# Last layer's half-heads on four PSUM banks of their own, read from the last state on; late operand parts loaded on SyncE's queue

## The chip, the cores and the metric

The kernel runs on one core of a Trainium2 chip. The metric is the time of one execution on the device in microseconds (us), the median over runs. TensorE (PE) multiplies matrices into PSUM, VectorE (DVE) and ScalarE (ACT) read and write PSUM and SBUF, GpSimd (POOL) does small vector work and issues DMAs, and SyncE (SP) only issues DMAs. Each engine works through its own list of instructions in order; semaphores tie the lists together.

## The reference

Two layers (DEPTH 2), 512 frames, width 2048, all in float32. Each layer is

```python
h = rmsnorm(x, g_pre)
z = h @ w_in          # gated linear attention q,k,v,gate,decay; chunk attention q,k,v,gate
...
S_c = diag(a_c) * S_(c-1) + sum over the chunk of decay * k_s v_s^T    # 8 chunks of 64 frames
o_gla = rmsnorm_per_head(q_c S_c) * silu(gg)                           # 4 heads, dk 128, dv 256
o_att = rmsnorm_per_head(chunk attention with bias) * silu(ag)         # 8 heads of 128
y = concatenate([o_gla, o_att]) @ w_out                                # 2048 x 2048
return x + rmsnorm(y, g_post)
```

The state recurrence runs over the chunks, and every frame of chunk c reads the state after its own chunk.

## The kernel before

**Products.** A float32 operand is split into a high and a low part (type fp32r), and each product takes three matmuls (high by high, high by low, low by high; L527 for the projections). A weight tile of 128x1024 comes by DMA into a buffer `raw` or `H` (L184, issued by SyncE), ACT casts its high part `wh` (L261), DVE subtracts for the low part `wl` (L267). There are four buffers each of `raw`, `H` and `wh` and three of `wl`, so the `wl` of one weight tile can be made only when PE is done with the tile three places earlier. Two column blocks of 512 form a pair, whose 2x2 block product is computed in Strassen's way with seven products P1 to P7 in place of eight; each needs a sum of weight tiles (DVE L250 or L253) or a sum of activations (S1 to S4, L1508). One job is one product of one chunk of 256 rows of the inner dimension: 12 matmuls of 128x512.

**The end of the program.** The last layer's output projection consists of the pairs W01 and W23. Its order is fixed by hand: P1 of W23, P1 of W01, P2 of W23, P2 of W01, each over the four chunks in the order 2, 3, 0, 1 (`C_END`); then for W01 P5, a mix of P6 and P3, P7 and P4; then the same for W23. The P1s need only the attention half of the activations. The P2s need the gated linear attention for the first 256 frames, and P5 on need it for all frames and the sums S1 to S4.

**Units.** The gated linear attention is done in eight half-heads, called units here, u0 to u7 in this order of (head, half of the frames): (0,0), (1,0), (2,0), (3,0), (2,1), (3,1), (0,1), (1,1). A unit has six steps. `outer` (L1300): four products k by v of 128x256 on PE into two PSUM banks. `states` (DVE L1320, L1322): four steps of the recurrence out of these banks. `read` (L1338): four products of q by state into a third bank. `norm` (ACT L1348 squares, POOL L1353 and L586 the power). `gate` (DVE L1360). `turn`: four transposes on PE (L1370) into a fourth bank, scaled by ACT (L1381) and split into high and low (ACT L113, DVE L114). All PSUM banks for this come one by one from a ring of four (`aux`), which the attention's last steps use as well. `gla_line` (L1429) starts unit n+1 while unit n is being read; it is a generator, advanced by a number of steps after every job (`rate`).

**Sums.** For each of the four chunks, `paired_sums` (L1479) makes S1, S2, S4 and S3 on DVE (L1508) from the parts of the activations: `parts[c]` has three tiles that `load_parts` reads back from DRAM (L1474 two loads from the attention, L1477 one from the gated linear attention), and the fourth is what `turn` left in SBUF. Each sum is split (ACT L113, DVE L114). S1 and S3 stay in SBUF; S2 and S4 are written to DRAM by POOL (L1522) and read back by SyncE (L238) shortly before P6 and P3. Chunks 2 and 3 are the early ones, 0 and 1 the late ones. Sums may begin when the states of all eight units have been issued (L1486).

**Loads.** The early parts are loaded on SyncE's queue after P1 of W23, into buffers `sa`. The late parts are loaded on POOL's queue after the last P1 of W01, into the buffers `a110` to `a113`, which are free when PE has done that P1. The gains for the output's norm (L1584) are on POOL's queue as well.

**What opens P5.** P5 of W01 writes the two banks that P2 of W23 filled. So ACT squares these banks (L1594) and DVE multiplies them by the gain (L1597) before P5's first matmuls; and the first weight sum of P5 (L250, called opening in L249) is tied behind that multiplication.

**Order.** The program is written in one order and then placed: for each engine a scheduler chooses the next instruction by its own idea of the times, held back by `tc.issue_after` where the kernel says so. So an edit of the written order changes the order on an engine only by way of this scheduler, and what stands where is read from the finished lists.

Of the kernel before, what the change touches and what calls it, by code (L numbers as in the profile page):

```python
# [35 lines left out]
def hybrid_trunk(  # L36
# [13 lines left out]
    nc = tc.nc  # L50
# [842 lines left out]
    def layer(l):  # L893
# [380 lines left out]
        og, og_full, issued = {}, {}, {"outer": 0, "states": 0}  # L1274
# [3 lines left out]
        class Unit:  # L1278
# [10 lines left out]
            def outer(self):  # L1289
                h, p = self.h, self.p  # L1290
                hk = slice(h * P, (h + 1) * P)
                hv = slice((h % 2) * 256, (h % 2 + 1) * 256)
                self.ps_u = [aux(), aux()]
                nc.vector.memset(self.ps_u[0][:, 0:1], 0.0)
                mm = None
                for tt in (1, 0):
                    for cc in (1, 0):
                        r = slice(cc * 64, (cc + 1) * 64)
                        with tc.issue_after(mm) if mm else nullcontext():
                            mm = nc.tensor.matmul(  # L1300
                                self.ps_u[cc][:, tt * 256 : (tt + 1) * 256], kd[p][r, tt, hk], self.gv[p][r, tt, hv],
                                start=True, stop=True,
                            ).ins
                issued["outer"] += 1
# [24 lines left out]
            def read(self):  # L1329
                h, p = self.h, self.p  # L1330
                self.ps_o = aux()
                mm = None
                for tt in range(2):
                    for cc in range(2):
                        q = 2 * tt + cc
                        n = 4 * p + q
                        with tc.issue_after(mm) if paired and mm else nullcontext():
                            mm = nc.tensor.matmul(  # L1338
                                self.ps_o[cc * 64 : (cc + 1) * 64, tt * 256 : (tt + 1) * 256],
                                gqT[h // 2][:, h % 2, n * 64 : (n + 1) * 64], self.st[q],  # L1340
                                start=True, stop=True,
                            ).ins
# [15 lines left out]
            def gate(self):  # L1358
                for tt in range(2):
                    nc.vector.scalar_tensor_tensor(  # L1360
                        out=self.sg[:, tt, :], in0=self.ps_o[:, tt * 256 : (tt + 1) * 256],
                        scalar=self.r[:, tt : tt + 1], in1=self.sg[:, tt, :], op0=ALU.mult, op1=ALU.mult,
                    )

            def turn(self):
                h, p = self.h, self.p
                ps = aux()
# [59 lines left out]
        units_due = []  # L1427

        def gla_line():  # L1429
            n, older = 0, None  # L1430
            while n < 8 or older is not None:
# [10 lines left out]
                yield  # L1442
# [5 lines left out]
                yield  # L1448
                yield
# [4 lines left out]
                yield  # L1454
                if older is not None:
                    older.gate()
                    delayed.append([4, older.turn])
# [11 lines left out]
        def load_parts(c, tiles):  # L1469
            views = [z.bitcast(F32)[:, i, :] for z in tiles for i in range(2)]  # L1470
            parts[c] = views
            q = nc.sync if c in C_END[:2] else nc.gpsimd
            for half, z in ((0, views[0]), (1, views[1])):
                q.dma_start(  # L1474
                    z.rearrange("p (k n) -> p k n", k=2), of_att[l][c][:, :, half * 256 : (half + 1) * 256]
                )
            q.dma_start(views[2], of_gla[l][0, c])  # L1477

        def paired_sums():  # L1479
# [5 lines left out]
            def ready(name, c):  # L1485
                if issued["states"] < 8 or c not in og_full or c not in parts:  # L1486
# [151 lines left out]
        def paired_out():  # L1638
# [14 lines left out]
            def side(n):  # L1653
                def f(k, c):
# [3 lines left out]
                    if (n, k, c) == (0, "P1", C_END[3]):  # L1658
                        gains[2], gains[0] = load_gain(2, nc.gpsimd), load_gain(0, nc.gpsimd)
                        for i in range(2):  # L1660
# [151 lines left out]
```

## Time and profile before

| | before |
|---|---|
| median of three runs (lowest to highest) | 1629.56 us (1629.43 to 1633.03) |
| profiled execution, its own time | 1631.98 us |
| span of the profiled execution | 1630.2 us |
| mean granted clock of TensorE | 0.992 |
| instructions | 24390 |
| PE busy | 1589.9 us (98% of the span) |
| DVE busy | 1275.6 us (78%) |
| ACT busy | 934.5 us (57%) |
| the last layer's paired output projection and units | about 1360 us on |

The profiled execution took 2.42 us longer than the median; of its 1631.98 us, 1.8 us lie outside the span. The profile's page gives for every engine its busy time and share. Groups of instructions are named by engine, source line, and output and inputs by tile name, with the idle time that the engine had just before them and the engine or DMA that ended this idle time. A row of the timeline has the start, the duration in us, the engine, the line, the operation, the shapes, the count, and in square brackets the idle time before it with what ended it. In the timeline a float32 matmul of a unit counts as two.

### The profile page before, as it was taken

The page shows a single profiled execution, that of the slowest core. Times are in us where ns is not written, and L with a number is a line of the kernel's source. Part 1 is how long each engine was busy: PE and PEld are TensorE (multiplying, and loading weights), DVE is VectorE, ACT ScalarE, POOL GpSimd, SP SyncE. Part 2 cuts the span into 40 slices and gives each one's busy share as a digit, 9 for nine tenths or more (in the row PEclk, how much of TensorE's full clock was granted, in tenths as well). Part 3 has the DMA queues.
Part 4 walks back from the last instruction along what each step waited for, and adds up shares of the span by engine and source line. Part 5 has one row for each costly group of instructions (what it writes and reads, how often), then busy time and mean ns, then how long its engine had stood idle before and what let it go on. Part 6 is the DMA issues. An engine that isn't in the chain of part 4 may idle for free.

```text
span 1630.2 us, 24390 instructions
## 1 busy us (share of the span) xinstructions
PE 1589.9 (98%) x8770; PEld 1347.9 (83%) x8770; DVE 1275.6 (78%) x1590; ACT 934.5 (57%) x1540; POOL 176.5 (11%) x306
## 2 busy tenths in 40 slices
PE   9999999999999999999999999999999999996896
PEld 6777889999988877788878888899998887775675
DVE  6778876877876886688869887868688767769687
ACT  8565544556676535455776455446667665455453
POOL 1131000000001102310121100000000010021101
PEclk9999999999999999999999999999999999998999
DMA  9999966858867797998689987787596848956794
GB/s 376 346 338 342 331 229 242 296 184 315 286 220 263 250 347 246 348 372 329 255 293 331 352 312 267 259 268 274 192 301 219 287 149 289 387 177 238 261 339 168
DMA packets 146857, 459.70 MB, mean 282 GB/s; under 512 B 16188, under 2 KB 34628, under 8 KB 146736
## 3 DMA queue, kind: packets, MB, share of 16 engines
q1 hardware_dynamic: 124560, 381.86, 66.6%
q0 software_dynamic: 21600, 75.33, 12.3%
q8 instruction: 69, 1.13, 0.3%
q10 hardware_dynamic: 576, 0.95, 0.2%
q14 instruction: 52, 0.43, 0.1%
HBM read 392.23 MB, written 64.77 MB: 280 GB/s over the span
## 4 chain that ended last, share of the span: by engine, by line
PE 85%; issue 6%; DMA 5%; DVE 3%; ACT 1%; POOL 1%; SPq 0%; POOLq 0%; DVEq 0%; ACTq 0%
PE mm L527 49%; PE mm L512 20%; PE mm L398 5%; DMA raw<-in_w_dram 3%; PE ax L1128 2%; DMA H<-in_w_dram 1%; DVE wl L267 1%; PE ax L1111 1%; PE ax L1338 1%; PE ax L1300 1%; PE ax L527 1%; PE ax L721 1%; PE ax L1091 1%; PE ax L1090 1%; PE ax L1089 1%
## 5 line engine op out<-in xcount | busy, mean ns | idle before, releaser
L267 DVE TENSOR_TENSOR wl<-raw,wh 128x1024 fp32r<-128x1024 f32 x248 | 302.8, 1222 | 119.7 <-PE mm L527 42.6
L261 ACT CAST wh<-H 128x1024 fp32r<-128x1024 f32 x251 | 263.5, 1052 | 224.2 <-PE mm L527 101.9
L261 ACT CAST wh<-raw 128x1024 fp32r<-128x1024 f32 x248 | 260.9, 1052 | 217.1 <-PE mm L527 98.0
L267 DVE TENSOR_TENSOR wl<-H,wh 128x1024 fp32r<-128x1024 f32 (+1 forms) x253 | 307.6, 1218 | 88.9 <-PE mm L527 35.3
L527 PE MATMUL mm<-wh,sa 128*128 128x512 f32 x1088 | 348.0, 394 | 5.2 <-DMA sa<-oS 4.6
L527 PE MATMUL mm<-wh,g 128*128 128x512 f32 x928 | 290.3, 392 | 6.5 <-ACT wh L261 6.1
L527 PE MATMUL mm<-wh,a 128*128 128x512 f32 x864 | 278.1, 395 | 2.3 <-ACT pc L450 0.9
L527 PEld LDWEIGHTS mm<-wh,sa 128*128 128x128 f32 x1088 | 203.9, 188 | 51.0 <-issue 7.5
L250 DVE TENSOR_TENSOR H<-H,raw 128x1024 f32<-128x1024 f32 x176 | 213.5, 1220 | 29.0 <-DMA raw<-in_w_dram 19.5
L512 PE MATMUL mm<-sa,wh 128*128 128x256 f32 x1280 | 235.9, 285 | 0.0
L527 PE MATMUL mm<-wl,sa 128*128 128x512 f32 x544 | 213.4, 392 | 0.0
L527 PEld LDWEIGHTS mm<-wh,g 128*128 128x128 f32 x928 | 175.2, 189 | 43.5 <-ACT wh L261 6.4
L512 PEld LDWEIGHTS mm<-sa,wh 128*128 128x128 f32 x1280 | 199.4, 191 | 0.3
L527 PEld LDWEIGHTS mm<-wh,a 128*128 128x128 f32 x864 | 160.9, 188 | 42.3 <-issue 5.8
L527 PE MATMUL mm<-wl,g 128*128 128x512 f32 x464 | 182.7, 394 | 11.4 <-DVE wl L267 11.4
L512 PE MATMUL mm<-sa,wl 128*128 128x256 f32 x640 | 180.8, 283 | 0.0
L527 PE MATMUL mm<-wl,a 128*128 128x512 f32 x432 | 169.7, 394 | 1.2 <-DVE wl L267 1.2
L512 PEld LDWEIGHTS mm<-sa,wl 128*128 128x128 f32 x640 | 122.3, 191 | 0.1
L527 PEld LDWEIGHTS mm<-wl,sa 128*128 128x128 f32 x544 | 102.6, 189 | 22.1 <-issue 0.7
L527 PEld LDWEIGHTS mm<-wl,g 128*128 128x128 f32 x464 | 87.6, 189 | 34.4 <-DVE wl L267 16.2
L527 PEld LDWEIGHTS mm<-wl,a 128*128 128x128 f32 x432 | 81.2, 188 | 20.6 <-DVE wl L267 3.0
L512 PE MATMUL mm<-a,wh 128*128 128x256 f32 x512 | 94.5, 285 | 0.0
(229 smaller groups left out, 2027.9 us busy)
## 6 DMA issues: line engine op xcount, KB each, us to landing
raw<-in_w_dram SPq DMA_DIRECT2D x356, 512.0 KB, 5.4
sa<-S SPq DMA_DIRECT2D x128, 512.0 KB, 4.6
H<-in_w_dram SPq DMA_DIRECT2D x67, 512.0 KB, 6.1
S<-g POOLq DMA_DIRECT2D x32, 512.0 KB, 6.2
g<-S SPq DMA_DIRECT2D x32, 512.0 KB, 5.9
sa<-A SPq DMA_DIRECT2D x32, 512.0 KB, 6.0
sa<-oS SPq DMA_DIRECT2D x32, 512.0 KB, 4.8
oS<-g POOLq DMA_DIRECT2D x24, 512.0 KB, 4.4
```

What stands on the lines that cost most here:

```text
L250: nc.vector.tensor_tensor(out=h, in0=h, in1=r, op=ALU.add)
L261: last_cast[0] = nc.scalar.copy(self.wh, src).ins
L267: last_low[0] = nc.vector.tensor_tensor(out=self.wl[:, kk, :], in0=self.src[:, kk, :], in1=self.wh[:, kk, :].bitcast(F32), op=ALU.subtract ...
L398: mm = nc.tensor.matmul(pss[o], a[:, part, t], rhs[:, kk, :], start=(i == 0 and kk == 0 and m == 0), stop=(i == n - 1 and kk == 1 and m == 2),
L512: nc.tensor.matmul(dst, lhs[:, kk, f], a[:, part, tok], start=(fresh and kk == 0 and m == 0 and ft % 2 == 0), stop=(c == self.last and kk ...
L527: mm = nc.tensor.matmul(out_ps[t], a[:, part, tok], rhs[:, kk, :], start=(fresh and kk == 0 and m == 0), stop=(c == self.last and kk == 1 ...
L721: mm = nc.tensor.matmul(gate_ps[l][g : g + 32, half * 256 : (half + 1) * 256], gate_w[l][:, kh * 8 + c * 2 + kk, :], full[half, c][:, kh, ...
L1089: nc.tensor.matmul(ps[:, :n], self.qh[:, t], self.kh[:, :n], start=True, stop=False)
L1090: nc.tensor.matmul(ps[:, :n], self.qh[:, t], self.kl[:, :n], start=False, stop=False)
L1091: nc.tensor.matmul(ps[:, :n], self.ql[:, t], self.kh[:, :n], start=False, stop=True)
L1111: nc.tensor.transpose(ps[:, j * P : (j + 1) * P], self.prob[i][:, j * P : (j + 1) * P], ident)
L1128: nc.tensor.matmul(o, self.pt[i][:, j * P : (j + 1) * P], av[hd // 4, j // 2][:, j % 2, (hd % 4) * P : (hd % 4 + 1) * P], start=(j == 0), ...
```

## The change

Five edits, all in the last layer only, the paired one (`paired` is true there); the lists of the first layer keep their order.

1. **Banks.** Once all four pairs of attention heads are done, `gla_line` takes the whole ring of four auxiliary banks for good. Banks 0 and 1 take every unit's `outer`, bank 2 or 3, by turns, its `read`, and `turn` transposes back into the bank that it was read into. So a unit's `outer` waits for the states of the unit before it, and no unit waits for another user of the ring.
2. **Read order.** `read` goes through the states 3, 2, 1, 0. Its first matmul needs the unit's last state, and the other three need nothing more.
3. **Steps.** Where there is no newer unit to start, `gla_line` leaves out the idle steps that belong to it, and the last `turn` follows its gate after 2 steps and not 4.
4. **Late parts.** The late parts are loaded on SyncE's queue like the early ones, and the loads are written after the first P2 job of W01 and not after the last P1 job.
5. **Sums.** They may begin when the gates of all eight units have been issued, not their states.

```diff
-        og, og_full, issued = {}, {}, {"outer": 0, "states": 0}
+        og, og_full, issued = {}, {}, {"outer": 0, "states": 0, "gates": 0}
...
-                self.ps_u = [aux(), aux()]
+                self.ps_u = gla_banks[:2] if paired else [aux(), aux()]
...
             def read(self):
                 h, p = self.h, self.p
-                self.ps_o = aux()
+                self.ps_o = gla_banks[2 + self.i % 2] if paired else aux()
                 mm = None
-                for tt in range(2):
-                    for cc in range(2):
-                        q = 2 * tt + cc
+                for q in (3, 2, 1, 0) if paired else range(4):
+                    tt, cc = divmod(q, 2)
...
+                issued["gates"] += 1

             def turn(self):
                 h, p = self.h, self.p
-                ps = aux()
+                ps = self.ps_o if paired else aux()
...
-        units_due = []
+        units_due, gla_banks = [], []

         def gla_line():
             n, older = 0, None
+            while len(heads_done) < 4:
+                yield
+            gla_banks.extend(aux() for _ in range(4))
             while n < 8 or older is not None:
...
                 yield
-                yield
+                if newer is not None:
+                    yield
                 if older is not None:
                     older.read()
                 yield
                 if newer is not None:
                     newer.states()
-                yield
-                yield
+                    yield
+                    yield
                 if older is not None:
                     older.norm()
                 yield
                 yield
-                yield
+                if newer is not None:
+                    yield
                 if older is not None:
                     older.gate()
-                    delayed.append([4, older.turn])
+                    delayed.append([4 if newer is not None else 2, older.turn])
...
-            q = nc.sync if c in C_END[:2] else nc.gpsimd
             for half, z in ((0, views[0]), (1, views[1])):
-                q.dma_start(
+                nc.sync.dma_start(
...
-            q.dma_start(views[2], of_gla[l][0, c])
+            nc.sync.dma_start(views[2], of_gla[l][0, c])
...
-                if issued["states"] < 8 or c not in og_full or c not in parts:
+                if issued["gates"] < 8 or c not in og_full or c not in parts:
...
                     if (n, k, c) == (0, "P1", C_END[3]):
                         gains[2], gains[0] = load_gain(2, nc.gpsimd), load_gain(0, nc.gpsimd)
+                    if (n, k, c) == (0, "P2", C_END[0]):
                         for i in range(2):
                             load_parts(C_END[2 + i], [slot(tag, [2, 512], F32R) for tag in (f"a11{2 * i}", f"a11{2 * i + 1}")])
```

In the changed kernel the same operations have other line numbers: `read` is L1337 and no longer L1338, `gate` L1359, the part loads L1478 and L1481 (L1474 and L1477 before), the sums L1512 (L1508), their writes L1526 (L1522), the gain loads L1588 (L1584), the multiplication by the gain L1601 (L1597), the squares L1598 (L1594).

The first place is PE around u2 and u3, in the last pair of the input projection, shortly ahead of P1 of W23. In the names `ax` is a unit's bank, `g_2813` and its like a unit's decayed keys, and `g_2695` the tile `ends`, which holds the last state of each unit of the first half. Before, u2's outer and the first product of u3's stand together, one projection matmul follows, then the rest of u3's:

```order
L1300 MATMUL ax_14050<-g_2813_14045,g_2664_13381 128x256
L1300 MATMUL ax_14049<-g_2813_14045,g_2664_13381 128x256
L1300 MATMUL ax_14050<-g_2813_14045,g_2664_13381 128x256
L1300 MATMUL ax_14049<-g_2813_14045,g_2664_13381 128x256
L1300 MATMUL ax_14085<-g_2813_14045,g_2664_13381 128x256
L527 MATMUL mm_13717<-wh_14039,sa_14043 128x512
L1300 MATMUL ax_14084<-g_2813_14045,g_2664_13381 128x256
L1300 MATMUL ax_14085<-g_2813_14045,g_2664_13381 128x256
L1300 MATMUL ax_14084<-g_2813_14045,g_2664_13381 128x256
L527 MATMUL mm_13717<-wl_14074,sa_14043 128x512
L527 MATMUL mm_13717<-wh_14039,sa_14043 128x512 x2
L527 MATMUL mm_13717<-wl_14074,sa_14043 128x512
```

After, from u3's outer on:

```order
L1300 MATMUL ax_13710<-g_2809_14041,g_2664_13381 128x256
L1300 MATMUL ax_13709<-g_2809_14041,g_2664_13381 128x256
L1300 MATMUL ax_13710<-g_2809_14041,g_2664_13381 128x256
L1300 MATMUL ax_13709<-g_2809_14041,g_2664_13381 128x256
L1337 MATMUL ax_13711<-g_2695_13517,g_2614_13146 64x256
L1337 MATMUL ax_13711<-g_2810_14044,g_2614_13146 64x256 x3
L527 MATMUL mm_13722<-wh_14071,sa_14075 128x512
L527 MATMUL mm_13722<-wl_14105,sa_14075 128x512
L527 MATMUL mm_13722<-wh_14071,sa_14075 128x512 x2
L527 MATMUL mm_13722<-wl_14105,sa_14075 128x512
L527 MATMUL mm_13722<-wh_14071,sa_14075 128x512
L1337 MATMUL ax_13712<-g_2695_13517,g_2614_13146 64x256
```

Behind it, u3's outer is whole, u2's read follows directly, and u3's read follows six projection matmuls later (one row counts two of them) with the product that needs the last state in front. Over all eight units, seven of these groups of four were cut by other instructions before (`outer` of u3, u4 and u6, `read` of u1, u4, u5 and u7), and one is after (`outer` of u6). u7's `turn` stood last ahead of P5; after, 39 projection matmuls stand between it and P5.

The second place is DVE at the start of P5 of W01, up to the first low weight part of P5 that PE waits for. In the names `mm_14396` and `mm_14397` before, and `mm_14374` and `mm_14375` after, are the two banks of W23's P2, `mm_14578` and `mm_14579` (`mm_14550` and `mm_14551`) those of W01's P2; a row with `H` and `raw` is a weight sum, and the last row is P5's first `wl`. Before, directly behind the two L1597 that read W23's banks:

```order
L250 TENSOR_TENSOR H_14366<-H_14366,raw_14768 128x1024
L1508 TENSOR_TENSOR sa_14416<-sa_14416 128x512
L250 TENSOR_TENSOR H_14414<-H_14414,raw_14799 128x1024
L1508 TENSOR_TENSOR sa_14462<-sa_14462 128x512
L250 TENSOR_TENSOR H_14460<-H_14460,raw_14822 128x1024
L1508 TENSOR_TENSOR a_2964_14660<-a_2964_14660 128x512
L250 TENSOR_TENSOR H_14528<-H_14528,raw_14845 128x1024
L114 TENSOR_TENSOR g_2971_14684<-a_2965_14661,g_2971_14684 128x512
L1597 TENSOR_TENSOR g_3007_14870<-mm_14578,t_2963_14658 128x512
L1597 TENSOR_TENSOR g_3009_14874<-mm_14579,t_2963_14658 128x512
L114 TENSOR_TENSOR g_2944_14572<-t_2945_14573,g_2944_14572 128x512
L267 TENSOR_TENSOR wl_14817<-H_14366,wh_14797 128x1024
```

After:

```order
L114 TENSOR_TENSOR g_2906_14498<-t_2907_14499,g_2906_14498 128x512
L1601 TENSOR_TENSOR g_2949_14706<-mm_14374,t_2934_14628 128x512
L1601 TENSOR_TENSOR g_2952_14712<-mm_14375,t_2934_14628 128x512
L250 TENSOR_TENSOR H_14357<-H_14357,raw_14702 128x1024
L1512 TENSOR_TENSOR sa_14394<-sa_14394 128x512
L1512 TENSOR_TENSOR t_2897_14457<-a_2957_14735,t_2897_14457 128x512
L1512 TENSOR_TENSOR t_2907_14499<-a_2959_14740,t_2907_14499 128x512
L250 TENSOR_TENSOR H_14392<-H_14392,raw_14733 128x1024
L1512 TENSOR_TENSOR sa_14433<-sa_14433 128x512
L250 TENSOR_TENSOR H_14431<-H_14431,raw_14779 128x1024
L250 TENSOR_TENSOR H_14486<-H_14486,raw_14817 128x1024
L267 TENSOR_TENSOR wl_14774<-H_14357,wh_14731 128x1024
```

And the rows that follow it, up to P5's second `wl`, where before one L114 stood between the two:

```order
L1512 TENSOR_TENSOR a_2957_14735<-a_2957_14735 128x512
L114 TENSOR_TENSOR a_2961_14746<-sa_14394,a_2961_14746 128x512
L1601 TENSOR_TENSOR g_2979_14842<-mm_14550,t_2935_14630 128x512
L114 TENSOR_TENSOR g_2962_14750<-t_2897_14457,g_2962_14750 128x512
L1601 TENSOR_TENSOR g_2981_14846<-mm_14551,t_2935_14630 128x512
L1512 TENSOR_TENSOR a_2959_14740<-a_2959_14740 128x512
L114 TENSOR_TENSOR g_2963_14754<-t_2907_14499,g_2963_14754 128x512
L267 TENSOR_TENSOR wl_14812<-H_14392,wh_14777 128x1024
```

Between the first of the two multiplications and the first `wl`, twelve operations stood before and nine after; between the first and the second `wl`, one before and seven after. The first sums (L1512) still stand ahead of the gates of u6 and u7 in DVE's list, as before.

The third place is SyncE's queue during the P2s. `sa` takes the early parts, `a` the late parts, `raw` a weight tile. After:

```order
L1481 DMA sa_14434<-fg_191 128x512
L1478 DMA a_2959_14740<-fa_177 128x2x256 x2
L1481 DMA a_2960_14741<-fg_189 128x512
L184 DMA raw_14622<-in_w_dram 128x1024
L1478 DMA a_2957_14735<-fa_176 128x2x256 x2
L184 DMA raw_14648<-in_w_dram 128x1024
L1481 DMA a_2958_14736<-fg_188 128x512
L184 DMA raw_14666<-in_w_dram 128x1024
L184 DMA raw_14684<-in_w_dram 128x1024
```

The four rows with `a` (two of them hold two loads each) stood on POOL's queue before, behind nothing but each other and the units' norms; they now stand among the weight loads. Each must wait for PE to be done with the P1 job that used its buffer.

More of the change, by code (lines that the diff above doesn't have):

```diff
@@ L1330, in read @@
                 h, p = self.h, self.p
-                self.ps_o = aux()
+                self.ps_o = gla_banks[2 + self.i % 2] if paired else aux()
                 mm = None
-                for tt in range(2):
-                    for cc in range(2):
-                        q = 2 * tt + cc
[L1336 to L1342, printed above, removed]
+                for q in (3, 2, 1, 0) if paired else range(4):
+                    tt, cc = divmod(q, 2)
+                    n = 4 * p + q
+                    with tc.issue_after(mm) if paired and mm else nullcontext():
+                        mm = nc.tensor.matmul(
+                            self.ps_o[cc * 64 : (cc + 1) * 64, tt * 256 : (tt + 1) * 256],
+                            gqT[h // 2][:, h % 2, n * 64 : (n + 1) * 64], self.st[q],
+                            start=True, stop=True,
+                        ).ins
             def norm(self):
```

## Prediction

> **What bounds the kernel now.** I read the page first, for the engine with no slack.
>
> ```profile
> PE 85%; issue 6%; DMA 5%; DVE 3%; ACT 1%; POOL 1%; SPq 0%; POOLq 0%; DVEq 0%; ACTq 0%
> ```
>
> PE holds 85% of the chain that ended last, and by the table above it is hardly ever idle. So time can come only from PE's few idle stretches and from PE's own rows. The view of waits, for PE from 1360 us on, the part that the change touches, lists these stretches (total, times, longest):
>
> ```profile
> PE mm L527 <- DVE wl L267: 9.9, 4, 6.4
> PE mm L527 <- ACT wh L261: 6.1, 1, 6.1
> PE mm L527 <- DMA sa<-oS: 4.6, 1, 4.6
> ```
>
> Two waits on DVE and ACT make up 12.6 of some 21 us. The timeline of PE shows where:
>
> ```profile
> 1481.16 0.60 PE L1370 MATMUL ax<-cst,sg 128*128 128x128 f32 x4
> 1487.88 1.22 PE L527 MATMUL mm<-wh,g 128*128 128x512 f32 x2 [6.12 <-ACT wh L261]
> 1495.55 0.79 PE L527 MATMUL mm<-wl,g 128*128 128x512 f32 x1 [6.45 <-DVE wl L267]
> ...
> 1500.16 0.39 PE L527 MATMUL mm<-wl,g 128*128 128x512 f32 x1
> 1500.38 0.39 PE L527 MATMUL mm<-wh,g 128*128 128x512 f32 x1
> 1500.61 0.39 PE L527 MATMUL mm<-wl,g 128*128 128x512 f32 x1
> ...
> 1526.22 0.47 PE L527 MATMUL mm<-wh,sa 128*128 128x512 f32 x1 [4.59 <-DMA sa<-oS]
> ```
>
> P2 of W01 ends with u7's turn at 1481.76; P5 opens 6.12 us later, runs two matmuls, and waits 6.45 us more. Then PE is slow for a while: the 12 matmuls from 1495.55 to 1500.16 take 4.61 us, where at the pace behind 1500.16 (0.45 for two; over whole jobs 0.2275 each) they would take 2.73. The third stop, 4.59 us, is P6's first late operand, which comes back from DRAM. The timeline of DVE tells why the first two are there:
>
> ```profile
> 1484.32 1.29 DVE L1597 TENSOR_TENSOR g<-mm,t 128x512 f32<-128x512 f32 x2 [1.95 <-DMA t<-in_g_post_dram]
> 1485.53 1.21 DVE L250 TENSOR_TENSOR H<-H,raw 128x1024 f32<-128x1024 f32 x1
> ...
> 1494.28 1.22 DVE L267 TENSOR_TENSOR wl<-H,wh 128x1024 fp32r<-128x1024 f32 x1
> ```
>
> The multiplications that free P5's banks start 2.6 us after P2's end, because their gains land late; the first low part of a weight ends only at 1495.5, twelve operations later. From start to start DVE needs 0.60 us for 128x512 (two from 1484.32 to 1485.53) and, as each row ends some 0.08 behind the next one's start, 1.13 for 128x1024. So what counts is when DVE comes to L1597, and how much stands between it and P5's `wl`s.
>
> **The change, part by part.** I call the end of W01's P2 T0: 1481.76 before.
>
> Banks and read order, ahead of T0. The projections go on at 0.2275 us a matmul; what differs is how the units' products lie between them. A group of four that is cut costs more than a whole one:
>
> ```profile
> 1454.60 0.70 PE L1300 MATMUL ax<-g,g 64*128 64x256 f32 x2
> ...
> 1455.65 1.13 PE L1300 MATMUL ax<-g,g 64*128 64x256 f32 x6
> ...
> 1460.14 1.13 PE L1300 MATMUL ax<-g,g 64*128 64x256 f32 x8
> ```
>
> Cut, 0.70 + 1.13 us; whole, 1.13. The 0.70 overlaps the next row by some 0.08, as above, which leaves 0.6 us a cut; a whole group takes 1.05. The order has seven cuts before and one after: -3.6 us. Against that stands a new wait. u3's read now begins with the last state and stands early. The nearest rows are those of the same units before:
>
> ```profile
> 1401.55 1.56 PE L1300 MATMUL ax<-g,g 64*128 64x256 f32 x10
> ...
> 1405.82 0.42 DVE L1320 COPY g<-ax 128x256 f32<-128x256 f32 x1
> 1406.27 1.51 DVE L1322 SCALAR_TENSOR_TENSOR g<-g,a_end,ax 128x256 f32<-128x256 f32 x3
> 1407.70 0.75 DVE L463 SCALAR_TENSOR_TENSOR g<-mm,norm,ev 128x512 f32<-128x512 f32 x1
> 1408.36 1.22 DVE L267 TENSOR_TENSOR wl<-H,wh 128x1024 fp32r<-128x1024 f32 x1
> ```
>
> u2's states are done when u3's copy starts, at 1405.82. Behind them DVE now does L463, a `wl`, L463, the copy, an L250 and three states: 0.66 + 1.13 + 0.66 + 0.45 + 1.13 + 1.43 = 5.5, so u3's last state is there at 1411.3. PE comes from 1401.55 over u2's outer (1.05), 18 matmuls (4.1), u3's outer (1.05), u2's read (as many products, 1.0) and 6 matmuls (1.4) to 1410.1: a wait of 1.2. The units behind it have their own read 27 or more matmuls (6 us) after their outer, against about 2.0 for four states and some 3 for what stands ahead of them on DVE, so I count no wait there. Together -2.4, with -3.6 and 0 as bounds; T0 moves to about 1479.3.
>
> P5's two stops. DVE's order now: the `wl` of the last P2 job can begin when PE has 36 matmuls left, T0 - 8.2, and ends at T0 - 7.1. Then come L114 (which I let wait 0.7 for ACT, a row like that is below), two L1601, L250, three L1512, L250, L1512, two L250 and P5's first `wl`: 0.7 + 0.6 + 1.2 + 1.13 + 1.8 + 1.13 + 0.6 + 2.26 + 1.2 = 10.6. That is T0 + 3.5. The first `wh` comes after the first L250, ahead of T0, so PE does two matmuls (0.45) and stops for 3.1, or 2.4 without the wait for ACT.
>
> ```profile
> 1479.13 1.09 POOL L1584 DMA_DIRECT2D t<-in_g_post_dram  x2
> 1479.58 0.69 DVE L114 TENSOR_TENSOR g<-t,g 128x512 fp32r<-128x512 f32 x1 [0.69 <-ACT g L113]
> 1476.81 0.88 DVE L1360 SCALAR_TENSOR_TENSOR sg<-ax,sm,sg 128x256 f32<-128x256 f32 x2 [0.61 <-POOL sm L586]
> ```
>
> Here the gains must be early. Before, POOL issued them at 1479.13, 2.3 us behind u7's gate, and DVE had them 5.2 us later. Now three `wl`s of P2 stand between u7's gate and L1601, and the first of them can begin at T0 - 8.2 - 2 x 2.73 = T0 - 13.7. So the gate starts by T0 - 14.5, and at the same distances, 2.3 + 5.2, the gains land at T0 - 7.0, 1.2 before L1601 wants them. Without that cover up to the old 1.95 is back.
>
> Up to the second `wl` stand seven operations of 0.60 and itself, 5.4: T0 + 8.9. PE does 10 matmuls and two of the next job, to T0 + 6.25, and stops for 2.65. The third `wl` (1.7 later) is in time, the fourth (4.1 after that, T0 + 14.7) is 0.3 late. Stops 3.1 + 2.65 + 0.3 = 6.05 against 12.57; for two or three short ones while the sums of the late chunks run beside P6 I add 1.1. -5.4, bounds -7 and -3.
>
> The slow stretch cost 4.61 - 2.73 = 1.9 before.
>
> ```profile
> 1480.00:1500.00 20.00, 7.44 (x24) 5.32 (x23) 17.98 (x24) 11.72 (x22) 1.83 (x4) 0.66 0.94 314
> 1561.39 0.50 PE L527 MATMUL mm<-wl,g 128*128 128x512 f32 x1 [1.92 <-DVE wl L267]
> 1561.97 0.39 PE L527 MATMUL mm<-wl,g 128*128 128x512 f32 x1
> ```
>
> The window has a granted clock of 0.66. After the stops of 6.45 and 4.59 the rows are slow, after one of 1.92 they are not. Stops of 3.1 and 2.65 lie between, and I take half of it: -1.0. The Trainium skill, in "TensorE: Matmul & The Clock Gate", Part 1, says that the clock halves after at least one idle window of about 3.4 us, which runs freely; the three stops agree with it. By that rule neither new stop would halve the clock and the term would be -1.9.
>
> P6's late operand. DVE's part for chunk 0 of S2 is done 6.9 us after the fourth `wl`, at T0 + 21.6.
>
> ```profile
> 1513.32 0.69 DVE L114 TENSOR_TENSOR g<-t,g 128x512 fp32r<-128x512 f32 x1
> 1514.30 0.54 POOL L1522 DMA_DIRECT2D oS<-g  x1 [20.91 <-DVE g L114]
> ```
>
> From the end of that operation (1514.0) over DRAM to PE's start at 1526.22 it took 12.2 us. So PE gets it at T0 + 33.8; it comes there after eight jobs of 2.73 and 7 us of stops, T0 + 28.8. A stop of 5.0 against 4.59; I take 0, with -1.8 and +2 as bounds. Behind it, in P7 and in W23, the order of sums and jobs changes a little; the waits there (1.92 in 1561.39 is the largest) may change either way: +0.7, from -1 to +3.
>
> Late parts on SyncE and fewer steps: I count 0 for them, covered by the weight buffers; the price without that cover is the second rival.
>
> Sum: -2.4 - 5.4 - 1.0 + 0 + 0.7 = -8.1. The profiled execution would take 1631.98 - 8.1 = 1623.9; it lies 2.42 above the median of 1629.56, so on that basis 1621.5.
>
> **The rivals.** *More.* All bounds on the good side: T0 by 1.2 more, no slow stretch (0.9), the DRAM trip shorter by 1.8: -12.0, 1617.5. For it speaks that the stops of the sum lie close under the ones that slowed the clock; against it that three things must come together.
>
> *The weights come late.* The late parts' loads wait for PE, and SyncE's weights stand behind them. On POOL they waited four times, from the first of these rows to the last:
>
> ```profile
> 1441.65 1.52 POOL L1474 DMA_DIRECT2D a<-fa  x2 [3.01 <-PE mm L527]
> ...
> 1452.43 0.57 POOL L1477 DMA_DIRECT2D a<-fg  x1 [1.40 <-PE mm L527]
> ```
>
> The page has the landing of a weight, 5.4 us from its issue:
>
> ```profile
> raw<-in_w_dram SPq DMA_DIRECT2D x356, 512.0 KB, 5.4
> ```
>
> At most 3.01 at a time, at most 12 in all. Four buffers are four jobs, 10.9 us; landing (5.4), `wl` (1.22) and at most as much for `wh` take 7.8, which leaves 3.1, just more than the longest wait. If half of the 12 reached PE, -8.1 + 6 = -2.1: 1627.5, no change.
>
> *Given back.* The operations taken from ahead of P5 aren't gone, and DVE is full again in P6 and P7. If the trip costs 2 more and the waits behind it 3 in place of 0.7: -3.8, 1625.8, no change that can be told.
>
> *Slower.* Each unit's outer now needs the two banks that the last unit's states are read from, and each read its last state. If not only u3 but the other seven made PE wait, at u3's 1.2 that is +8.4, about 0 in all; it decides from 1.9 us a unit on (8.1 + 4.9, divided by 7), and at 2.5, the chain of copy and three states with one L463 ahead (0.45 + 1.43 + 0.66), the kernel takes 1629.56 - 8.1 + 17.8 = 1639.3. For it speaks that each DVE chain starts only when DVE comes to it; against it the 6 us between outer and read for the other units.
>
> *It doesn't do what it says.* The first sums stand ahead of u6's and u7's gates in DVE's list after the change too. If what follows P2 lasted as before, only T0 would move: -2.4, 1627.2.
>
> **How the numbers follow.** A measurement of this kernel can tell about 0.3%, 4.9 us, from no change. Forecast 0.60, more 0.13, weights late 0.06, given back 0.11, not what it says 0.04, slower 0.06. Faster by over 0.3% are the first two and a little of the given back: 0.76; slower only one: 0.06; the rest 0.18. The range, 1615 to 1628, takes in the bounds of the sum up to the late weights and leaves out the slower case and the far end of "more".
>
> **What would show it.** PE's stops at the start of P5: 3 and 2.7, released by `wl`, and none by `wh`; no wait of L1601 for its gain; one new wait of about 1.2 at u3's read (L1337) and no others at L1337 or L1300; a clock near 1 in the 20 us behind T0; the stop for `sa` from `oS` still 4 to 5. A wait of P2's matmuls for a weight's DMA, or a stop of over 5 at P5, would prove the sum wrong.

## The result and the profile after

| | before | after |
|---|---|---|
| median, us (4 runs each) | 1630.22 | 1618.22 |
| lowest to highest, us | 1629.43 to 1633.03 | 1618.17 to 1619.01 |
| profiled execution, us (span) | 1631.98 (1630.2) | 1618.17 (1616.4) |

The ratio is 0.9924, with an interval of 0.9907 to 0.9942: the kernel is 12.0 us faster. The two profiled executions differ by 13.8. To see where, I use four marks: the landmark, which lies ahead of the change, is the last turn of the attention heads (L1159); T0 is the end of W01's P2, where after the change P5's first matmul starts; then come P5's fifteenth matmul and the last projection matmul. PE's timeline of before has these rows that were not shown yet:

```profile
1342.91 0.60 PE L1159 MATMUL ax<-cst,sg 128*128 128x128 f32 x4
...
1617.92 0.39 PE L527 MATMUL mm<-wh,g 128*128 128x512 f32 x1
```

PE's timeline after, from the landmark to the last projection matmul:

```profile
1341.24 0.60 PE L1159 MATMUL ax<-cst,sg 128*128 128x128 f32 x4
...
1405.06 0.47 PE L527 MATMUL mm<-wh,sa 128*128 128x512 f32 x1 [1.73 <-DMA sa<-A]
...
1411.48 1.08 PE L1337 MATMUL ax<-g,g 128*64 128x256 f32 x8 [1.14 <-DVE g L1322]
...
1468.15 0.60 PE L1370 MATMUL ax<-cst,sg 128*128 128x128 f32 x4
...
1477.45 0.61 PE L527 MATMUL mm<-wh,g 128*128 128x512 f32 x2
1481.34 0.50 PE L527 MATMUL mm<-wl,g 128*128 128x512 f32 x1 [3.28 <-DVE wl L267]
...
1483.23 1.06 PE L527 MATMUL mm<-wh,g 128*128 128x512 f32 x2
1484.08 0.63 PE L527 MATMUL mm<-wl,g 128*128 128x512 f32 x1
1484.51 1.46 PE L527 MATMUL mm<-wh,g 128*128 128x512 f32 x3
1486.68 0.50 PE L527 MATMUL mm<-wl,g 128*128 128x512 f32 x1 [0.72 <-DVE wl L267]
...
1508.66 0.47 PE L527 MATMUL mm<-wh,sa 128*128 128x512 f32 x1 [1.42 <-DMA sa<-oS]
...
1513.93 0.47 PE L527 MATMUL mm<-wh,sa 128*128 128x512 f32 x1 [2.30 <-DMA sa<-oS]
...
1604.20 0.39 PE L527 MATMUL mm<-wh,g 128*128 128x512 f32 x1
```

P5 now opens at 1477.45 with no stop. u7's turn, which stood last ahead of P5, runs 9.3 us ahead of it, at 1468.15. The two long stops at the opening, 6.12 and 6.45, have become 3.28 and 0.72. The table gives the start of each mark in both executions, and the distance; the prediction's share is in the last column.

| stretch | before | after | change | predicted |
|---|---|---|---|---|
| up to the landmark | 1342.91 | 1341.24 | -1.7 | - |
| landmark to P5 (T0) | 138.85 | 136.21 | -2.6 | -2.4 |
| P5's first 14 matmuls, with their stops | 18.40 | 9.23 | -9.2 | -7.8 |
| from P5's fifteenth matmul to the last | 117.76 | 117.52 | -0.2 | +2.1 |
| from there to the span's end | 12.28 | 12.20 | -0.1 | 0 |

The first row lies ahead of all that was changed, so 12.1 of the 13.8 belong to the change, as the medians say. Of the prediction's sum of -8.1, the stops of 3.1 and 2.65 in place of 12.57 (-6.8) and the clock (-1.0) fall into the 14 matmuls, and the 0.3, 1.1 and 0.7 that it put on top fall behind them.

PE's waits after, from 1340 us on (total, times, longest; the two smallest rows are left out), show the same from the other side:

```profile
PE mm L527 <- DVE wl L267: 6.7, 7, 3.3
PE mm L527 <- DMA sa<-oS: 3.7, 2, 2.3
PE mm L527 <- DMA sa<-A: 1.7, 1, 1.7
PE ax L1337 <- DVE g L1322: 1.1, 1, 1.1
```

The wait for `wh` is gone; one wait at u3's read and one for `sa` from `A` are new, and there is none at L1300. DVE's timeline after, at P5's opening, to set beside that of before:

```profile
1469.29 1.23 DVE L267 TENSOR_TENSOR wl<-raw,wh 128x1024 fp32r<-128x1024 f32 x1 [1.94 <-PE mm L527]
1471.32 0.69 DVE L114 TENSOR_TENSOR g<-t,g 128x512 fp32r<-128x512 f32 x1 [0.80 <-ACT g L113]
1471.93 1.28 DVE L1601 TENSOR_TENSOR g<-mm,t 128x512 f32<-128x512 f32 x2
1473.12 1.21 DVE L250 TENSOR_TENSOR H<-H,raw 128x1024 f32<-128x1024 f32 x1
...
1480.07 1.21 DVE L267 TENSOR_TENSOR wl<-H,wh 128x1024 fp32r<-128x1024 f32 x1
...
1485.42 1.21 DVE L267 TENSOR_TENSOR wl<-H,wh 128x1024 fp32r<-128x1024 f32 x1
```

L1601 waits for nothing and starts 5.5 us ahead of T0, where L1597 started 2.6 behind it. The first two `wl`s end at T0 + 3.8 and T0 + 9.2; the prediction had T0 + 3.5 and + 8.9.

### The profile page after: what moved, and what is told of

Read it like the earlier page. It is cut to its first block, busy times and chain, and to the rows that moved or that the text cites. A ratio compares the mean times of both kernels' runs of the same rounds, so it can differ in the third digit from the quotient of the medians.

```text
span 1616.4 us, 24395 instructions
## 1 busy us (share of the span) xinstructions
PE 1584.1 (98%) x8770; PEld 1344.4 (83%) x8770; DVE 1274.6 (79%) x1590; ACT 931.7 (58%) x1540; POOL 172.2 (11%) x300
## 3 DMA queue, kind: packets, MB, share of 16 engines
q8 instruction: 69, 1.13, 0.3%
## 4 chain that ended last, share of the span: by engine, by line
PE 88%; issue 4%; DVE 3%; DMA 3%; ACT 1%; POOL 0%; SPq 0%; POOLq 0%; DVEq 0%
PE mm L527 52%; PE mm L512 20%; PE mm L398 5%; PE ax L1128 2%; DMA raw<-in_w_dram 2%; DVE wl L267 1%; DMA H<-in_w_dram 1%; PE ax L1111 1%; PE ax L1300 1%; PE ax L1337 1%; DVE H L250 1%; PE ax L527 1%; PE ax L721 1%; PE ax L1090 1%; PE ax L1091 1%
## 5 line engine op out<-in xcount | busy, mean ns | idle before, releaser
L267 DVE TENSOR_TENSOR wl<-raw,wh 128x1024 fp32r<-128x1024 f32 x248 | 302.5, 1220 | 108.6 <-PE mm L527 37.2
L267 DVE TENSOR_TENSOR wl<-H,wh 128x1024 fp32r<-128x1024 f32 (+1 forms) x253 | 307.2, 1217 | 86.0 <-PE mm L527 33.7
L250 DVE TENSOR_TENSOR H<-H,raw 128x1024 f32<-128x1024 f32 x176 | 213.5, 1220 | 24.2 <-DMA raw<-in_w_dram 14.9
```

The source lines that it names most:

```text
L250: nc.vector.tensor_tensor(out=h, in0=h, in1=r, op=ALU.add)
L267: last_low[0] = nc.vector.tensor_tensor(out=self.wl[:, kk, :], in0=self.src[:, kk, :], in1=self.wh[:, kk, :].bitcast(F32), op=ALU.subtract ...
```

## The experiments

*Theory A*: the whole gain comes from banks and read order together. The units' groups lie on PE in fewer pieces, and the units are done earlier, which lets DVE begin P5's chain ahead of T0. *Rivals*: the part loads do it, by clearing POOL's queue for the gains, so that these land in time (G); or one of the two unit edits is enough. Two of the five edits need no run. With the steps (edit 3), the condition on the sums (edit 5) or both put back, the lists of all five engines are the same, instruction for instruction: these two do nothing here.

**Loads back on GpSimd (e1_banks_read_only).** The changed kernel without edit 4.

```diff
+            q = nc.sync if c in C_END[:2] else nc.gpsimd
...
-                nc.sync.dma_start(
+                q.dma_start(
...
-            nc.sync.dma_start(views[2], of_gla[l][0, c])
+            q.dma_start(views[2], of_gla[l][0, c])
...
-                    if (n, k, c) == (0, "P2", C_END[0]):
```

> The changed kernel with the late part loads back on GpSimd's queue behind the P1s (edit 4 undone), so the four banks and the read order alone. Theory A (whole groups on PE, and u7's turn early enough that VectorE reaches P5's opening ahead of P2's end): PE's list is nearly that of the changed kernel, first low part nine operations behind the first multiplication by the gain, so about 6 us lost at P5's opening as in the changed kernel, 1618 to 1620 us. Theory B (the gain comes from the queues: GpSimd no longer held by the late loads): most of the 12 us is lost again, 1625 us or more.

Measured: 1616.37 us, ratio to before 0.9901 (0.9884 to 0.9918). The changed kernel on another chip (below) has 0.9917 (0.9904 to 0.9930), so the loads' edit has no effect that can be told. The profile is of the fastest of the five executions, 1612.30 us, while the slowest took 1616.98. PE's waits from 1340 us on:

```profile
PE mm L527 <- DVE wl L267: 6.6, 3, 4.6
PE mm L527 <- DMA sa<-oS: 2.5, 1, 2.5
PE ax L1337 <- DVE g L1322: 1.1, 1, 1.1
```

**The loads alone (e2_loads_only).** The kernel before with edit 4 only (`nc.sync.dma_start` for all parts, and the loads written after P2's first job).

```diff
-                q.dma_start(
+                nc.sync.dma_start(
...
-            q.dma_start(views[2], of_gla[l][0, c])
+            nc.sync.dma_start(views[2], of_gla[l][0, c])
...
+                    if (n, k, c) == (0, "P2", C_END[0]):
```

> The kernel before with the late part loads on SyncE's queue behind the first P2 job (edit 4 alone). Theory A: u7's turn still stands last ahead of P5, the multiplications by the gain still start 2.6 us behind P2's end, and 12 operations still stand ahead of the first low part; the chain is 0.6 us shorter: 1629 to 1630 us. Theory B: half of the gain or more, 1624 us or less.

Measured: 1632.34 us, ratio 1.0002 (0.9993 to 1.0011). PE's stops at P5 stay at 6.85 and 5.85, and DVE still waits for the gains:

```profile
1485.34 1.29 DVE L1596 TENSOR_TENSOR g<-mm,t 128x512 f32<-128x512 f32 x2 [6.78 <-DMA t<-in_g_post_dram]
```

**The states read forward (e3_read_forward).** The changed kernel without edit 2.

```diff
-                for q in (3, 2, 1, 0) if paired else range(4):
+                for q in range(4):
```

> The changed kernel with the states read in the order 0 to 3 (edit 2 undone). The scheduler then cuts the units' products on PE into 50 pieces in place of 30 (40 before). Theory A: each further piece costs 0.3 to 0.6 us of PE, 6 to 12 us in all ahead of P5, nothing behind it: 1624 to 1630 us. Theory C (cuts cost nothing, the gain ahead of P5 is something else): 1618 us.

Measured: 1631.27 us, ratio 1.000 (0.999 to 1.001): the whole gain is gone. The opening stays short, with one stop of 4.99, but T0 comes late. From the landmark (1342.64) to P5's first matmul it takes 145.97, 9.8 more than in the changed kernel:

```profile
1488.61 0.63 PE L527 MATMUL mm<-wh,g 128*128 128x512 f32 x2
1494.22 0.79 PE L527 MATMUL mm<-wl,g 128*128 128x512 f32 x1 [4.99 <-DVE wl L267]
```

**Banks from the ring (e4_ring_banks).** The changed kernel without edit 1.

```diff
-                self.ps_u = gla_banks[:2] if paired else [aux(), aux()]
+                self.ps_u = [aux(), aux()]
...
-                self.ps_o = gla_banks[2 + self.i % 2] if paired else aux()
+                self.ps_o = aux()
...
-                ps = self.ps_o if paired else aux()
+                ps = aux()
...
-            while len(heads_done) < 4:
-                yield
-            gla_banks.extend(aux() for _ in range(4))
```

> The changed kernel with the units' banks from the common ring as before (edit 1 undone). 35 pieces on PE, and u7's turn again directly ahead of P5. Theory A: about 2 us less ahead of P5 than before and 0.6 at P5's opening, 1627 to 1628 us. Theory B (loads) or one by which the read order alone does it: 1622 us or less.

Measured: 1628.72 us, ratio 0.9982 (0.9973 to 0.9992). Here it is the other way round: T0 is early, 135.5 us behind the landmark (1341.69), but u7's turn stands directly ahead of P5 again, and both stops are back:

```profile
1476.61 0.60 PE L1370 MATMUL ax<-cst,sg 128*128 128x128 f32 x4
1484.65 1.22 PE L527 MATMUL mm<-wh,g 128*128 128x512 f32 x2 [7.43 <-ACT wh L261]
1491.72 0.79 PE L527 MATMUL mm<-wl,g 128*128 128x512 f32 x1 [5.85 <-DVE wl L267]
```

So the read order gives T0 and the banks give the opening; the read order without the banks is worth 1.8 us by the medians, and the banks without the read order nothing. The four kernels also size the groups. In PE's list I count the pieces, rows of a unit's products of one kind (outer, read or turn) with nothing else between, the five turns at the start of the last layer with them: 30 after and in e1, 35 in e4, 40 before, 50 in e3. The distance from landmark to P5, without the stops in it, is 133.3 after (136.21 - 1.73 - 1.14), 135.3 (135.5 without one stop of 0.2), 138.3 (138.85 without one of 0.5) and 145.3 (145.97 without stops of 0.5 and 0.2): 0.6 us a piece from 30 to 50.

**The gains on SyncE (e5_gains_on_sync).** The kernel before with its two gain loads on the queue that is not late.

```diff
-                        gains[2], gains[0] = load_gain(2, nc.gpsimd), load_gain(0, nc.gpsimd)
+                        gains[2], gains[0] = load_gain(2), load_gain(0)
```

> The kernel before, with the two gains that P5's opening needs loaded on SyncE's queue instead of GpSimd's. Theory G (the gains' late landing is what holds VectorE at P5's opening): the wait of 1.95 us for the gain goes; two low-part splits still stand ahead of the multiplication, so 0 to 2 us less: 1628 to 1630 us. Theory T (u7's late turn holds it, the gain only seems to): no change, 1630 us.

Measured: 1629.52 us, ratio 0.9994 (0.9985 to 1.0002). The wait for the gain is gone from DVE, and PE's stops are still 5.57 and 5.85. DVE comes to L1597 no earlier than 2.0 us behind T0 (1480.42), because its own list ahead of it lasts up to there. ACT's first square ends hardly earlier, at 1482.39:

```profile
1481.83 0.69 DVE L114 TENSOR_TENSOR g<-a,g 128x512 fp32r<-128x512 f32 x1 [0.80 <-ACT g L113]
1482.44 1.28 DVE L1597 TENSOR_TENSOR g<-mm,t 128x512 f32<-128x512 f32 x2
```

**Loads and gains on SyncE (e6_loads_and_gains_on_sync).** The edits of e2 and e5 together. In e2 the sums no longer stand ahead of L1596, and DVE waited 6.78 us for nothing but the gain; with the gain early, theory G has its best case.

```diff
-                q.dma_start(
+                nc.sync.dma_start(
...
-                        gains[2], gains[0] = load_gain(2, nc.gpsimd), load_gain(0, nc.gpsimd)
+                        gains[2], gains[0] = load_gain(2), load_gain(0)
```

> The kernel of the run with the loads alone on SyncE (e2), with the gains there too. In e2 VectorE sat idle for 6.8 us ahead of P5's opening, waiting for the gain, and PE lost 6.85 + 5.85 us. Theory G: the chain starts 6.8 us earlier, the first low part is there 6.6 us behind P2's end in place of 12.7 and the rest of the opening keeps pace: about 6 us less than e2, 1624 us. Theory T: u7's turn, still directly ahead of P5, holds the opening whatever the gain does: 1629 us or more.

Measured: 1630.26 us, ratio 0.9999 (0.9991 to 1.0008). Theory G falls, and three timelines say why. SyncE's queue issues the gains early:

```profile
1474.68 1.42 SPq L1583 DMA_DIRECT2D t<-in_g_post_dram  x2
```

ACT comes to the squares late:

```profile
1482.35 0.84 ACT L1381 ACTIVATE t<-ax,gcol 128x256 f32<-128x256 f32 x2 [5.81 <-PE ax L1370]
1483.08 0.59 ACT L1593 ACTIVATE t<-mm 128x512 bf16<-128x512 f32 x1
```

And DVE waits for these:

```profile
1483.80 1.29 DVE L1596 TENSOR_TENSOR g<-mm,t 128x512 f32<-128x512 f32 x2 [4.96 <-ACT t L1593]
```

The gains are issued 9 us ahead of the multiplication, and DVE waits all the same, now for ACT. ACT's list has the scaling of u7's turned output (L1381) ahead of the squares that the multiplication needs (L1593), and the scaling waits 5.81 us for u7's turn on PE, the last thing ahead of P5. So u7's turn holds the opening, over ACT and DVE, though neither the multiplication nor P5's first jobs read anything that comes from it (only P5's last job, chunk 1, does, through S1). After the change ACT has the same two lines in the same order, 8.7 us ahead of T0 and not just behind it:

```profile
1468.78 0.84 ACT L1381 ACTIVATE t<-ax,gcol 128x256 f32<-128x256 f32 x2 [1.42 <-PE ax L1370]
1469.51 0.60 ACT L1598 ACTIVATE t<-mm 128x512 bf16<-128x512 f32 x1
```

**S3's sums on GpSimd (e7_s3_on_gpsimd).** In the changed kernel the stop of 3.28 is released by a `wl` with sums ahead of it in DVE's list. This kernel gives S3's sums and low parts to GpSimd.

```diff
-    def split(hi, lo, src):
+    def split(hi, lo, src, eng=nc.vector):
...
-        nc.vector.tensor_tensor(out=lo, in0=src, in1=hi.bitcast(F32), op=ALU.subtract)
+        eng.tensor_tensor(out=lo, in0=src, in1=hi.bitcast(F32), op=ALU.subtract)
...
+                eng = nc.gpsimd if name == "S3" else nc.vector
...
-                    nc.vector.tensor_tensor(out=out, in0=in0, in1=in1, op=op)
+                    eng.tensor_tensor(out=out, in0=in0, in1=in1, op=op)
...
-                    split(z[:, 0, :], z[:, 1, :], out)
+                    split(z[:, 0, :], z[:, 1, :], out, eng)
```

> The changed kernel with the four S3 sums and their low parts on GpSimd, which idles there. Theory D (PE waits at P5 for nothing but VectorE's list): two operations fewer ahead of the first low part and three fewer ahead of the second, stops of about 2.1 and 0.8 in place of 3.3 and 0.7 plus a slow clock; the return of S2 earlier too: 3 to 5 us less than the changed kernel, 1613 to 1615 us. Rival: GpSimd slows VectorE down or delays its own puts and gains, and nothing is won: 1618 us or more.

Measured: 1619.92 us, ratio 0.9932 (0.9918 to 0.9946), where the change itself has 0.9917 on the same chip: theory D's 1613 to 1615 us do not come. POOL's timeline:

```profile
1476.84 3.82 POOL L1513 TENSOR_TENSOR a<-a 128x512 f32<-128x512 f32 x2 [10.13 <-issue]
```

DVE's, beside it:

```profile
1477.22 6.73 DVE L250 TENSOR_TENSOR H<-H,raw 128x1024 f32<-128x1024 f32 x3
1483.87 2.28 DVE L267 TENSOR_TENSOR wl<-H,wh 128x1024 fp32r<-128x1024 f32 x1
```

And PE's:

```profile
1486.21 0.79 PE L527 MATMUL mm<-wl,g 128*128 128x512 f32 x1 [8.10 <-DVE wl L267]
```

DVE has fewer instructions and takes longer: beside GpSimd's sums (1.9 us each, DVE does one in 0.68) three L250 take 6.73 us, where at 1.13 apart they take 3.5, and the `wl` takes 2.28, not 1.21. These four cost 4.3 us more, and two operations fewer save only 1.2. L1602, which has one input in PSUM, keeps its 0.68 us beside GpSimd's work (at 1487.76). Another part of the loss stands ahead of GpSimd's sums: L1602 starts at 1473.68, 1.75 us later than in the changed kernel, after a wait of 1.63 for its gain. Together PE's stop grows from 3.28 to 8.10. The stops for `sa` from `oS` are gone, and one of 2.76 for a `wl` is new in W23, so the total is close to that of the change.

**The change again (e8_changed_again).** The changed kernel as it is, without any edit, on the chip of e5 to e7.

> The changed kernel itself once more, as the base of the other runs on this chip: 1618 us. If the late loads on SyncE cost 1 to 2 us, as the difference to the run without them (e1) hints, it stays above e1's 1616.4.

Measured: 1616.93 us, ratio 0.9917 (0.9904 to 0.9930). In this profile there is no stop for `sa` from `A`; from the landmark (1343.04) to P5 (1477.06) it takes 134.02, 4.8 less than before. The opening is as in the first profile: one stop of 3.29, and the fifteenth matmul 9.24 behind T0. The second stop of 0.72 is not there at all: PE works at half its pace from the restart up to the fifteenth matmul, and the `wl` is ready when PE comes to it.

**A turn written later (e9_turn_written_later).** The changed kernel with the last units' turns, the ones behind which no newer unit is waiting, written 30 steps after their gate and not 2. This moves other work of PE, ACT and DVE ahead of them. In this kernel and the next a unit's turn can overwrite the bank into which the unit two later was read, before that unit's gate reads it, so the attention output of such a unit is not the reference's; kind and amount of the work are the same.

```diff
-                    delayed.append([4 if newer is not None else 2, older.turn])
+                    delayed.append([4 if newer is not None else 30, older.turn])
```

> The changed kernel with u7's turn written 30 steps behind its gate in place of 2, which lets the scheduler place the first multiplication by the gain ahead of the last P2 low part and P5's first low part some three operations earlier; PE's list ends with u7's turn 51 matmuls ahead of P5 (39 before). Theory T (ScalarE's squares stand behind the scaling of u7's turn, so the place of that turn on PE sets when P5 opens): the first low part is there 0.5 us behind P2's end in place of 3.6, two or three stops of 1.4 follow, no slow clock; 3 us less than the changed kernel, 1613 to 1615 us. Rival (VectorE's total work sets the time up to P6's late operand, so what the opening wins is given back there): 1616 to 1618 us.

Measured: 1620.2 us, ratio 0.9934 (0.9916 to 0.9952). The six executions lie between 1615.74 and 1625.03, and the profile is of one of 1616.32. PE's timeline, at P5's opening and in P6:

```profile
1476.40 0.50 PE L527 MATMUL mm<-wl,g 128*128 128x512 f32 x1 [0.65 <-DVE wl L267]
...
1515.56 0.77 PE L527 MATMUL mm<-wh,sa 128*128 128x512 f32 x1 [10.10 <-DMA sa<-oS]
```

The multiplications by the gain start at 1465.86, 6 us earlier than in the changed kernel, and the stop at the opening shrinks from 3.28 to 0.65. P6's late operand then makes PE wait 10.10 in place of 3.7. So theory T is right about the opening, and its 1613 to 1615 us do not come: the rival, that the gain is given back, holds.

**The same without the loads' edit (e10_turn_later_loads_on_gpsimd).** The line of e9 in the kernel of e1.

```diff
-                    delayed.append([4 if newer is not None else 2, older.turn])
+                    delayed.append([4 if newer is not None else 30, older.turn])
```

> The same written turn with the late loads back on GpSimd (the kernel of e1 with the turn 30 steps behind its gate). Theory T: the same early opening, 1613 to 1615 us; the loads' queue makes no difference of over 1 us. Rival as for e9: 1616 us, as e1.

Measured: 1619.15 us, ratio 0.9927 (0.9914 to 0.9940). The stop at the opening is 2.83 (4.60 in e1), that for P6's operand 5.29 (2.48 in e1). What is won at P5's start is owed in P6, and here too the 1613 to 1615 us do not come. No kernel tried is faster than the change by more than the intervals.

## Why the prediction was right, and what it mis-sized

The time predicted was 1621.5 and the time is 1618.2; the range holds it, and places and releasers were those of the likeliest case. The number itself lies nearer to the rival *more* (1617.5) than to the forecast, and some terms are right only because their errors cancel. The steps one by one:

**T0.** -2.4 predicted, -2.6 in the first profile, but by two errors that cancel. The new wait at u3's read was 1.14 (1.2 predicted). The groups saved more than 3.6: I counted cut groups of `outer` and `read` only, 7 to 1, and left out the turns, which are cut as well. In pieces it is 40 to 30, and at 0.6 each 6; measured are 138.3 - 133.3 = 5.0. Against it stood a stop of 1.73 for `sa` from `A` that I had not foreseen. It is not there in e8, where T0 comes 4.8 us earlier than before. Why this operand was late in one execution I cannot say.

**P5's two stops.** Place, releaser and order were right: `wl`, not `wh`, at the matmuls named. The first stop was 3.28 (3.1 predicted). The second was 0.72 and not 2.65, because the clock was slow between the two: of the 2.65 that DVE needed, 1.93 passed while PE worked at half its pace.

**The slow clock.** I took half of 1.9, and it came in full, but behind a wait that would have been there anyway. That is the failed step of the sum: stops and slow clock were added, though here the slow PE only used up the wait that followed it (0.72 us left of it in the first profile, nothing in e8). In before the same slow stretch had no wait behind it and cost its 1.9. I also left out 0.6 that before lost on P5's first two matmuls (1.22 for the two, 0.61 after). The window of P5's opening after (PE, PEld, DVE, ACT, POOL, clock, DMA, GB/s):

```profile
1480.00:1500.00 20.00, 17.09 (x64) 12.95 (x65) 20.00 (x26) 12.81 (x19) 0.31 (x1) 0.91 0.37 137
```

A clock near 1 was the sign I had named, and it is 0.91. DVE, 20.00 of 20, now sets the pace there.

**Behind it.** +2.1 predicted (short stops at P5 and later waits), -0.2 measured. For `sa` from `oS` there are two stops of 3.7 in all in place of one of 4.59, and in this execution neither is followed by slow rows, which saves 0.9 and the slow rows behind the old stop, some 1.5. That part is luck: in e8 the second of the two is shorter, and the rows behind it are slow (below). The waits behind that are eight and not four, and add up to 3.8 as before. Some 2 us go back in gaps of 0.1 to 0.4 that the view of waits doesn't list. I had counted only the losses, so this is the largest mis-sized term.

**Why the gains mattered less than I said.** I put L1597's late start in before down to its gains, as the trace does. They were only the last of three things to end. e5 takes them away, and DVE's own list, with ACT's squares close behind it, holds L1597 up to T0 + 2.0, where it was T0 + 2.6; e6 takes that list away as well, and ACT's squares, queued behind the scaling of u7's turn, hold it up to T0 + 1.5 (1483.80 - 1482.31). The size came out right because the change moves all three.

**The rivals.** *Weights late*: no wait of PE for a weight's DMA, and e1 and e8 show no difference for the loads. *Slower*: one unit waited, u3, for 1.14; the other seven did not. *Given back*: not in the change, but e9 and e10 show that the mechanism is real one step further on. *Not what it says*: u7's turn is 9.3 us ahead of P5. *More* (1617.5) has the size that was measured, though not by its terms: T0 came 0.2 earlier than forecast and not 1.2, the slow stretch was there, and the stops for `sa` from `oS` are still 3.7.

## What to carry to other kernels

A wait that a trace puts down to one transfer can have the next one right under it; here, with one after the other taken away, L1597 started 2.6, 2.0 and 1.5 us behind T0, and the root of the last was a chain whose data it doesn't need, tied in by one engine's order. Count every kind of group that is cut between long matmuls, at 0.6 us a piece here, and don't add a slow clock to a wait that comes after it. Work moved ahead on a full engine is owed later: ask of each operation what it now stands in front of.

## What the runs showed of the hardware

- **Shorter stops than I had thought can slow the clock, and their length alone does not decide.** Stops of 3.28 (after), 2.83 (e10) and 2.48 (e1) were followed by some 3 to 4 us in which two 512-wide matmuls took 1.05, not 0.62; stops of 2.30 (after), 1.76 (e3) and 1.42 (after) were not. PE's timeline of e1, in P6:

```profile
1509.99 0.47 PE L527 MATMUL mm<-wh,sa 128*128 128x512 f32 x1 [2.48 <-DMA sa<-oS]
...
1511.56 1.05 PE L527 MATMUL mm<-wh,sa 128*128 128x512 f32 x2
```

But in e8, the changed kernel again, a stop of only 1.97 at the place of the 2.30 was followed by such rows too:

```profile
1513.26 0.47 PE L527 MATMUL mm<-wh,sa 128*128 128x512 f32 x1 [1.97 <-DMA sa<-oS]
...
1514.86 1.06 PE L527 MATMUL mm<-wh,sa 128*128 128x512 f32 x2
```

The granted clock was 0.64 in the 4.8 us from this restart on, and 1.00 in the same stretch of the first profile, behind the 2.30. What else decides isn't shown here.

The Trainium skill, in "TensorE: Matmul & The Clock Gate", Part 1, asks for an idle window of about 3.4 us. By that rule the two stops of 3.1 and 2.65 that I forecast would have left the clock alone. The traces differ: the stops of 3.28, 2.83, 2.48 and 1.97 were all shorter and were followed by slow rows, so by the measurement one of about 2 us can be enough, and the two that I forecast were not safe.

- **GpSimd's sums slow VectorE.** In e7 a 128x1024 operation of DVE took 2.2 us, not 1.13, beside sums of GpSimd. The Trainium skill, in "GPSIMD Engine Reference", section 8, says that the two share their SBUF interfaces and contend when a VectorE instruction has two SBUF inputs. The trace agrees: L250 and L267 have two and were slowed, and L1602, with one of its two in PSUM, was not (0.68).
